# Summing weight blocks inside the transfer: accumulating loads in place of VectorE adds in a seven-product feed-forward

## The chip, the cores and the metric

The kernel runs on one core of one Trainium2 chip. The metric is the device time of one execution in microseconds (us). The granted clock of TensorE is given as a share of its full speed of 2.4 GHz.

## The reference

Two decoder layers over 256 tokens of width 2048, all in float32. Layer 0 has differential attention, layer 1 multi-head latent attention; each is followed by a dense SwiGLU feed-forward with 5632 hidden columns. Only the second product of the feed-forward matters for the change:

```
def _swiglu(h, w_in, w_out):
    g, u = jnp.split(h @ w_in, [FFN_HIDDEN], axis=-1)
    return (jax.nn.silu(g) * u) @ w_out

for i in range(DEPTH):
    ...
    y = _swiglu(_rmsnorm(x, g[2]), ffn_w_in[i], ffn_w_out[i])
    x = x + _rmsnorm(y, g[3])
```

## The kernel before

Each float32 product is made of three matmuls over a high and a low part (`mm3`, lines 94 to 100): high x high, high x low, low x high. A weight piece of 128 x 2048 float32 (1 MB) is loaded by SyncE and split in two halves by `split_weight` (lines 81 to 92): for each half ScalarE casts the high part (`whi`, line 103) and VectorE subtracts it to get the low part (`wlo`, line 104). The pools of `whi` and of `wlo` hold six halves each, so three pieces can be split or in use at one time; the pool of loaded pieces `w` holds two, that of raw output-weight blocks `wr` three.

In a feed-forward (`ffn`, from line 461) the hidden columns come in 11 blocks of 512. `block_in` projects one block: eight pieces of `win`, 24 matmuls each, and after each of them it yields. Blocks 0 to 9 form five pairs. For a pair and two groups of 512 output columns, `unit` (from line 555) computes a 2 x 2 product of blocks (two token tiles by two hidden blocks, times two hidden blocks by two column groups) with seven block products in place of eight. The sums on the side of the hidden values are the operands A11, S1, S2, S4, S3, A12 and A22; the sums on the side of the weights are made in the tiles t1 and t3:

```
t1 = W[b1,n1]                       product 1 (A11)
t1 += W[b1,n2]                      product 2 (S1)
t1 += W[b2,n2]                      product 3 (S2)
W[b2,n2] itself                     product 4 (S4)
t3 = W[b1,n2] + W[b2,n2]            product 5 (S3)
W[b2,n1] itself                     product 6 (A12)
t1 += W[b2,n1]                      product 7 (A22)
```

Each product is 12 matmuls of 512 columns. The raw blocks t1, t3, b22 and b21 are loaded by SyncE (`raw`, line 561). One step of a unit runs at each yield of `block_in`, so one projection piece and one product alternate on TensorE. There are two units to a pair and five pairs to a layer, 20 units in the kernel; the last unit of each layer runs when no block is left to project, among the products of the single eleventh block (lines 652 to 675).

The order of instructions on each engine is made by the planner when the kernel is built, from the order of the program and its own estimate of durations; on the chip each engine then takes its instructions in that order and waits where data or a buffer is missing. GpSimd does only the small steps of the norms (`rsqrt_mean`, lines 119 to 125) once its tables are made.

Of the kernel before, what the change touches and what calls it, by code (L numbers as in the profile page):

```python
# [14 lines left out]
ALU = mybir.AluOpType  # L15
# [24 lines left out]
def trunk_kernel(ctx: ExitStack, tc: tile.TileContext, a: dict):  # L40
    nc = tc.nc
# [39 lines left out]
    def split_weight(w, shape, parts=1):  # L81
        both = []
        half = shape[0] // 2
        for h in range(2):
            hi = whi.tile([P, half] + shape[1:], F32R, tag="whi", name="whi")
            lo = wlo.tile([P, half] + shape[1:], F32R, tag="wlo", name="wlo")
            n = half // parts
            for i in range(parts):
                c = slice(i * n, (i + 1) * n)
                split_to(hi[:, c], lo[:, c], w[:, h * half + i * n : h * half + (i + 1) * n])  # L90
            both += [(hi[:, i], lo[:, i]) for i in range(half)]
        return both
# [368 lines left out]
    def ffn(i, rstd, second_tokens, first_tokens, aside=None):  # L461
        win, wout = a[f"win{i}"], a[f"wout{i}"]
# [87 lines left out]
        def product(ps, lhs, rhs, more=False):  # L550

            for k in range(4):
                mm3(ps, (lhs[0][:, k], lhs[1][:, k]), rhs[k], not more and k == 0, k == 3, more)

        def unit(pair, X, cgs, first):

            (b1, b2), (n1, n2) = pair, cgs

            def raw(blk, cg):
                w = wr.tile([P, 4, CW], F32, tag="r", name="wr")  # L560
                nc.sync.dma_start(w, wout[blk, cg])
                return w

            def split(w):
                return split_weight(w, [4, CW])

            def add(into, w):
                nc.vector.tensor_tensor(into, into, w, op=ALU.add)  # L568

            def sums():  # L570
                return wp.tile([P, CW], F32, tag="wp", name="wp")

            def ys(t, cg):
                return y[:, t, cg * CW : (cg + 1) * CW]

            def gather(t, cg, ps, sign, fresh=False):
                if fresh:
                    nc.scalar.mul(ys(t, cg), ps, sign)
                else:
                    op = ALU.add if sign > 0 else ALU.subtract  # L580
                    nc.vector.tensor_tensor(ys(t, cg), ys(t, cg), ps, op=op)  # L581

            t1 = raw(b1, n1)
            pa = sums()
            product(pa, X["A11"], split(t1))
            gather(0, n1, pa, 1.0, first)
            yield
            t3 = raw(b1, n2)
            add(t1, t3)
            pc = sums()  # L590
            product(pc, X["S1"], split(t1))
            gather(1, n2, pc, -1.0, first)
            yield
            b22 = raw(b2, n2)
            add(t1, b22)
            product(pa, X["S2"], split(t1), more=True)
            gather(0, n2, pa, -1.0, first)
            yield
            product(pc, X["S4"], split(b22), more=True)
            gather(0, n2, pc, -1.0)  # L600
            yield
            add(t3, b22)
            product(pa, X["S3"], split(t3), more=True)
            gather(1, n2, pa, -1.0)
            yield
            b21 = raw(b2, n1)
            pc = sums()
            product(pc, X["A12"], split(b21))
            gather(0, n1, pc, 1.0)
            yield  # L610
            add(t1, b21)
            product(pa, X["A22"], split(t1), more=True)
            gather(1, n1, pa, 1.0, first)
            yield
# [17 lines left out]
        for blk in range(NBLK):  # L632
            if blk == NBLK - 1:
                A, hidden = single_operands()
            elif blk % 2 == 0:
                X, hidden, second = pair_operands()
            else:
                hidden = second
            for _ in block_in(blk, hidden):
                next(steps, None)  # L640
            drain(steps)
            if blk == 2 and aside is not None:
                aside()
            if blk % 2 == 1:
                waiting = (PAIRS[blk // 2], X, blk == 1)
                steps = unit(waiting[0], waiting[1], (0, 1), waiting[2])
            elif waiting is not None:
                steps = unit(waiting[0], waiting[1], (2, 3), waiting[2])
# [355 lines left out]
```

## Time and profile before

| | |
|---|---|
| median of three runs | 2126.69 us (2126.25 to 2127.41) |
| the profiled execution: its own time | 2126.84 us |
| its span, first to last instruction | 2125.1 us |
| TensorE busy | 2077.7 us (98%) |
| VectorE busy | 1584.2 us (75%) |
| ScalarE busy | 1123.2 us (53%) |
| GpSimd busy | 45.5 us (2%) |
| moved by DMA | 394.97 MB, mean 186 GB/s |

Busy time is the time in which an engine executes something; a share of the whole span hides that stages have different limits. In the chain of work that ended last, TensorE holds 92% of the span, VectorE 5% and DMA 2%.

### The profile page before, as it was taken

To read this page: it belongs to the slowest core of one execution; us is meant where nothing else is said; L and a number is where in the kernel's file an instruction comes from. 1 tells how busy PE (TensorE), PEld (TensorE's weight loads), DVE (VectorE), ACT (ScalarE), POOL (GpSimd) and SP (SyncE) were. 2 spreads that over 40 slices of the span, in tenths; PEclk is the share of its full clock that TensorE was granted. 3 is DMA by queue.
4 is the path that set the end of the run, shared out by engine and by line. 5 is a ranking of instruction groups with operands and counts; after the bars stand their busy time and mean duration, and the time that the engine had idled before them with its cause. 6 is when DMAs were issued, how large, how long until landed. Compare 5 with 4: busy or idle time off the path is not lost.

```text
span 2125.1 us, 26154 instructions
## 1 busy us (share of the span) xinstructions
PE 2077.7 (98%) x10348; PEld 1770.9 (83%) x10348; DVE 1584.2 (75%) x1757; ACT 1123.2 (53%) x1439; POOL 45.5 (2%) x83
## 2 busy tenths in 40 slices
PE   8999999999999999999998999999999999999997
PEld 7999998788888888888877898878888888888875
DVE  6655555657878888887887786475888878888887
ACT  6444444455555555555555654454555555555554
POOL 0000000000000000000001100000000000000000
PEclk9999999999999999999999999999999999999998
DMA  7555456454556555566534533645455556555552
GB/s 248 179 174 175 162 179 229 167 198 144 213 201 224 189 181 198 188 220 223 182 114 151 198 138 135 237 162 194 179 174 190 207 208 219 195 177 196 189 202 94
DMA packets 59452, 394.97 MB, mean 186 GB/s; under 512 B 7105, under 2 KB 7361, under 8 KB 13633
## 3 DMA queue, kind: packets, MB, share of 16 engines
q1 hardware_dynamic: 59328, 393.30, 53.0%
q8 instruction: 81, 1.33, 0.3%
q14 instruction: 43, 0.34, 0.0%
HBM read 391.17 MB, written 2.10 MB: 185 GB/s over the span
## 4 chain that ended last, share of the span: by engine, by line
PE 92%; DVE 5%; DMA 2%; issue 1%; ACT 1%; POOL 0%; SPq 0%; DVEq 0%; POOLq 0%; ACTq 0%
PE ps L98 24%; PE ps L100 24%; PE ps L99 24%; PE wp L99 5%; PE wp L100 5%; PE wp L98 5%; DVE wlo L104 2%; PE pt L494 1%; DVE x L262 1%; PE pt L110 1%; PE ps_s L863 0%; PE ps_s L389 0%; PE ps_s L864 0%; PE po L428 0%; ACT whi L103 0%
## 5 line engine op out<-in xcount | busy, mean ns | idle before, releaser
L104 DVE TENSOR_TENSOR wlo<-w,whi 128x1024 fp32r<-128x1024 f32 (+3 forms) x582 | 697.7, 1205 | 300.5 <-ACT whi L103 282.3
L103 ACT CAST whi<-w 128x1024 fp32r<-128x1024 f32 (+3 forms) x582 | 600.5, 1039 | 509.7 <-PE ps L100 246.6
L98 PE MATMUL ps<-whi,xTh 128*128 128x512 f32 (+2 forms) x1632 | 631.8, 390 | 1.3 <-ACT xTh L103 1.3
L99 PE MATMUL ps<-wlo,xTh 128*128 128x512 f32 (+2 forms) x1632 | 631.9, 387 | 0.0
L100 PE MATMUL ps<-whi,xTl 128*128 128x512 f32 (+2 forms) x1632 | 631.8, 387 | 0.0
L103 ACT CAST whi<-wr 128x1024 fp32r<-128x1024 f32 x280 | 293.2, 1051 | 302.0 <-PE ps L100 268.3
L104 DVE TENSOR_TENSOR wlo<-wr,whi 128x1024 fp32r<-128x1024 f32 x280 | 340.1, 1223 | 124.0 <-ACT whi L103 112.2
L98 PEld LDWEIGHTS ps<-whi,xTh 128*128 128x128 f32 x1632 | 308.3, 189 | 61.9 <-ACT xTh L103 2.4
L100 PEld LDWEIGHTS ps<-whi,xTl 128*128 128x128 f32 x1632 | 307.9, 189 | 60.4 <-DVE xTl L104 0.2
L99 PEld LDWEIGHTS ps<-wlo,xTh 128*128 128x128 f32 x1632 | 308.3, 189 | 59.9 <-DVE wlo L104 0.4
L568 DVE TENSOR_TENSOR wr<-wr 128x2048 f32<-128x2048 f32 x80 | 182.8, 2285 | 23.5 <-DMA wr<-in_wout 23.3
L98 PE MATMUL ps<-xTh,whi 128*128 128x256 f32 x512 | 146.8, 287 | 1.6 <-ACT whi L103 1.6
L100 PE MATMUL ps<-xTh,wlo 128*128 128x256 f32 x512 | 144.8, 283 | 0.8 <-DVE wlo L104 0.8
L99 PE MATMUL ps<-xTl,whi 128*128 128x256 f32 x512 | 144.8, 283 | 0.0
L98 PEld LDWEIGHTS ps<-xTh,whi 128*128 128x128 f32 x512 | 98.2, 192 | 2.2 <-ACT whi L103 2.0
L98 PE MATMUL ps<-whi,oTh 128*128 128x512 f32 x256 | 100.0, 393 | 0.0
L100 PE MATMUL ps<-whi,oTl 128*128 128x512 f32 x256 | 99.2, 390 | 0.0
L99 PE MATMUL ps<-wlo,oTh 128*128 128x512 f32 x256 | 99.2, 390 | 0.0
L100 PEld LDWEIGHTS ps<-xTh,wlo 128*128 128x128 f32 x512 | 98.1, 192 | 1.1 <-DVE wlo L104 1.0
L99 PEld LDWEIGHTS ps<-xTl,whi 128*128 128x128 f32 x512 | 98.2, 192 | 0.2
L581 DVE TENSOR_TENSOR y<-y,wp 128x512 f32<-128x512 f32 x124 | 84.4, 681 | 3.7 <-PE wp L100 3.7
L98 PE MATMUL wp<-whi,S_S 128*128 128x512 f32 x160 | 63.7, 398 | 5.7 <-ACT whi L103 5.7
(210 smaller groups left out, 2358.2 us busy)
## 6 DMA issues: line engine op xcount, KB each, us to landing
w<-in_win SPq DMA_DIRECT2D x176, 1024.0 KB, 4.9
wr<-in_wout SPq DMA_DIRECT2D x80, 1024.0 KB, 4.9
w<-in_wqk SPq DMA_DIRECT2D x32, 1024.0 KB, 4.9
w<-in_wo SPq DMA_DIRECT2D x32, 1024.0 KB, 4.9
w<-in_wv SPq DMA_DIRECT2D x15, 1024.0 KB, 4.9
w<-in_wout SPq DMA_DIRECT2D x8, 1024.0 KB, 5.1
w<-in_wdown SPq DMA_DIRECT2D x8, 724.0 KB, 4.3
g<-in_norm_gains SPq DMA_DIRECT2D x16, 256.0 KB, 3.6
```

The costliest lines, as they stand in the source:

```text
L98: nc.tensor.matmul(out, lh, rh, start=first, stop=False, skip_group_check=more)
L99: nc.tensor.matmul(out, lh, rl, start=False, stop=False, skip_group_check=more)
L100: nc.tensor.matmul(out, ll, rh, start=False, stop=last, skip_group_check=more)
L103: nc.scalar.copy(hi, src)
L104: nc.vector.tensor_tensor(lo, src, hi.bitcast(F32), op=ALU.subtract)
L110: nc.tensor.transpose(pt[:, j * P : (j + 1) * P], src[:, j * P : (j + 1) * P], ident)
L262: nc.vector.scalar_tensor_tensor(xs, y[:, t, cg * CW : (cg + 1) * CW], ry, xs, op0=ALU.mult, op1=ALU.add)
L494: nc.tensor.transpose(pt[:, j * P : (j + 1) * P], hs[t][:, j * P : (j + 1) * P], ident)
L568: nc.vector.tensor_tensor(into, into, w, op=ALU.add)
L581: nc.vector.tensor_tensor(ys(t, cg), ys(t, cg), ps, op=op)
```

## The change

The helper `add` in `unit` no longer adds one loaded tile into another on VectorE. It issues a transfer from GpSimd's queue that reads the block from memory and adds it to what the destination tile holds. The tiles that are also used by themselves (t1, t3, b22, b21) are still loaded as before, so the four blocks that enter a sum are read from memory once more for each sum.

```diff
-            def add(into, w):
-                nc.vector.tensor_tensor(into, into, w, op=ALU.add)
+            def add(into, blk, cg):
+
+                nc.gpsimd.dma_start(into, wout[blk, cg], accum_op=ALU.add)
...
             t3 = raw(b1, n2)
-            add(t1, t3)
+            add(t1, b1, n2)
...
             b22 = raw(b2, n2)
-            add(t1, b22)
+            add(t1, b2, n2)
...
-            add(t3, b22)
+            add(t3, b2, n2)
             product(pa, X["S3"], split(t3), more=True)
...
-            add(t1, b21)
+            add(t1, b2, n1)
             product(pa, X["A22"], split(t1), more=True)
```

## Rows read from the trace of the kernel before

**Rows 1.** The core's span and its mean granted clock.
```profile
core 0: 2125.1 us, clock 0.990
```
**Rows 2.** Busy time by stretch: a whole unit, and both layers' ends.
```profile
core 0: us, PE busy (x) PEld busy (x) DVE busy (x) ACT busy (x) POOL busy (x), PEclk, DMA share, GB/s
...
812.00:875.00 63.00, 63.00 (x283) 52.27 (x283) 51.78 (x46) 34.42 (x37) 0.00 (x0) 1.00 0.57 198
...
1062.00:1092.00 30.00, 26.40 (x107) 21.25 (x106) 26.15 (x25) 13.67 (x15) 0.00 (x0) 0.89 0.37 134
...
2052.00:2082.00 30.00, 26.40 (x114) 21.39 (x113) 26.59 (x24) 13.68 (x15) 0.00 (x0) 0.94 0.38 133
```
**Rows 3.** What TensorE waited for, 1060 to 1125: total, times, longest.
```profile
PE wp L98 <- ACT whi L103: 2.8, 1, 2.8
PE wp L99 <- DVE wlo L104: 0.8, 1, 0.8
```
**Rows 4.** The group of the adds on the page.
```profile
L568 DVE TENSOR_TENSOR wr<-wr 128x2048 f32<-128x2048 f32 x80 | 182.8, 2285 | 23.5 <-DMA wr<-in_wout 23.3
```
**Rows 5.** DMA from 812 to 875: queue, and issues with us to landing.
```profile
q1 hardware_dynamic: 1709, 12.43, 56.6%
...
w<-in_win SPq DMA_DIRECT2D x8, 1024.0 KB, 4.8
wr<-in_wout SPq DMA_DIRECT2D x4, 1024.0 KB, 4.8
```
**Rows 6.** Landing times of all 80 raw blocks (line 561).
```profile
DMA to landing us min/median/max: 4.7/4.9/11.8
```
**Rows 7.** Durations of GpSimd's small norm step, ns min/median/max.
```profile
L122 POOL TENSOR_SCALAR ms<-so x20: 190/274/3277, 89.2 to 1190.9; 128x1 f32<-128x1 f32 x20
```
**Rows 8.** VectorE in order of time, products 1 and 2 of a unit.
```profile
816.66 1.22 DVE L104 TENSOR_TENSOR wlo<-wr,whi 128x1024 fp32r<-128x1024 f32 x1
...
818.58 2.28 DVE L568 TENSOR_TENSOR wr<-wr 128x2048 f32<-128x2048 f32 x1
...
825.91 2.53 DVE L104 TENSOR_TENSOR wlo<-wr,whi 128x1024 fp32r<-128x1024 f32 x2
...
829.71 2.29 DVE L568 TENSOR_TENSOR wr<-wr 128x2048 f32<-128x2048 f32 x1
```
**Rows 9.** ScalarE: the first casts of products 2 and 3.
```profile
824.76 1.05 ACT L103 CAST whi<-wr 128x1024 fp32r<-128x1024 f32 x1 [3.07 <-PE ps L100]
...
833.82 1.05 ACT L103 CAST whi<-wr 128x1024 fp32r<-128x1024 f32 x1 [0.61 <-PE ps L100]
```
**Rows 10.** TensorE: the first matmuls of products 2 and 3.
```profile
834.93 0.39 PE L98 MATMUL wp<-whi,S_S 128*128 128x512 f32 x1
...
843.09 0.39 PE L98 MATMUL wp<-whi,S_S 128*128 128x512 f32 x1
```
**Rows 11.** VectorE at the end of the first layer.
```profile
1066.04 2.59 DVE L104 TENSOR_TENSOR wlo<-wr,whi 128x1024 fp32r<-128x1024 f32 x2 [2.48 <-ACT whi L103]
1068.66 2.29 DVE L568 TENSOR_TENSOR wr<-wr 128x2048 f32<-128x2048 f32 x1
...
1074.33 2.35 DVE L104 TENSOR_TENSOR wlo<-wr,whi 128x1024 fp32r<-128x1024 f32 x2
...
1080.13 2.28 DVE L568 TENSOR_TENSOR wr<-wr 128x2048 f32<-128x2048 f32 x1
```
**Rows 12.** TensorE there: products 2 and 3 of the last unit.
```profile
1076.99 0.39 PE L98 MATMUL wp<-whi,S_S 128*128 128x512 f32 x1
...
1083.60 0.50 PE L98 MATMUL wp<-whi,S_S 128*128 128x512 f32 x1 [2.84 <-ACT whi L103]
1084.86 0.79 PE L99 MATMUL wp<-wlo,S_S 128*128 128x512 f32 x1 [0.76 <-DVE wlo L104]
```
**Rows 13.** The chain that ended last, 1079 to 1092: start, us, piece.
```profile
1086.50 0.43 PE wp L99
...
1091.32 0.23 PE wp L99
```

## The prediction

> **What bounds the kernel now.** I read the cores first: one core, span 2125.1 us, granted clock 0.99 [rows 1], which is the upper level, 2.4 GHz, nearly throughout. Then the table by stretches. In a stretch of the first feed-forward layer that holds one whole seven-product unit, TensorE is busy 63.00 of 63 us at clock 1.00, VectorE 51.78, ScalarE 34.42, and the 16 DMA engines 0.57 of the time; of the stretches with units only those at the ends of the two layers leave TensorE short, 26.40 of 30 us each, at clock 0.89 and 0.94 [rows 2]. The reader is to see that VectorE's load is no bound in the middle of a layer: there is no time there that a lighter VectorE could give back. The waits of TensorE say what the ends cost: 2.8 us for a cast and 0.8 us for a subtraction in each [rows 3]. That and a stretch of matmuls at the lower clock level are all that this change can win.
>
> **What it removes.** 80 VectorE adds of 2.285 us, 182.8 us of VectorE [rows 4]; four in each of 20 units (5 pairs x 2 units x 2 layers). Of these units 18 run between the projection pieces of a block, and 2 (the last of each layer) run bare at a layer's end. In the middle the 9.1 us of adds per unit hide behind a TensorE that never waits, so removing them is worth 0 there; were VectorE the bound, it would be worth up to those 9.1 us a unit.
>
> **What it adds.** 80 transfers of 1 MB into a tile that already holds data, issued by GpSimd: 83.9 MB on top of 395 MB. One unit's stretch now carries 12 loads (8 and 4 of 1 MB) in 56.6% of 63 us [rows 5], so one load holds the 16 engines for 0.566 x 63 / 12 = 3.0 us, and lands 4.8 us after issue, 1.8 us of which is fixed. The trace has no accumulating transfer. Bounds of its latency L, from the last read of the tile to the sum being there: below, the fastest plain landing, 4.7 us, if the second operand costs nothing and GpSimd starts as fast as SyncE; above, the slowest plain landing, 11.8 us [rows 6], with a second operand (3.0) and GpSimd's slowest small instruction as its start (3.3, median 0.27) [rows 7]: 18.1 us. I take: fixed 1.8, engine time 6.0 (the old content of the tile has to be fetched as well as the block, so twice 3.0), 3.4 for other loads that get in meanwhile (0.566 of 6.0), and 1.0 for GpSimd's start: L = 12.2 us. I take twice, not once, because two operands of 1 MB must pass; nothing in the rows argues for more.
>
> In the Trainium skill, *Collectives: The Full Stack*, section "The bandwidth ceiling: the fold count and why AG ≠ RS ≠ AR", a reduction done by the DMA engines runs at half the rate of a copy since it reads two sources, and the addition itself costs nothing. No row here shows that; by it the 6.0 stands, by the plain row's 3.0 alone L would be 7.5 and the middle would cost nothing. *DMA: Bandwidth & Descriptors*, section "Measured (HBM→SBUF, 128 partitions, SWDGE, issued from GpSimd)", gives 6.15 us of engine span for 1 MB issued from GpSimd, descriptor writing not counted, against this trace's 4.8 from SyncE to landing. With that in place of 4.8, L would be 13.5 us and the end some 2279 us, as an estimate from that page, inside the forecast's own range below.
>
> **What waits for it.** The tile t1 holds the first, second, third and seventh weights in turn, so the second and third sums form a chain: subtraction of product 1's split ends, sum, split, sum, split. In the stretch above, product 1's split ends at 816.66 + 1.22 = 817.9, the adds run at 818.58 and 829.71, and the split between them subtracts from 825.91 to 828.44 [rows 8]. The casts of products 2 and 3 start at 824.76 and 833.82 [rows 9]; their first matmuls at 834.93 and 843.09 [rows 10], one step of 8.16 us apart. From a cast's start to the end of the first half's subtraction is 2.4 us (824.76 to 827.2), to the end of the second half's 3.7 (to 828.44). So there is cover: the splits run ahead of TensorE by most of a step. With sums that land L after the last read, product 3 can start on time if 817.9 + L + 3.7 + L + 2.4 is no later than 843.3 (its second matmul is the first to need a subtracted half), so if 2L is at most 19.3, L at most 9.65 us. Product 2 alone would bear L = 14.8. The last add on t1, product 7's, has four more steps and stays hidden; so does the one into t3, which no earlier product reads.
>
> At L = 12.2 each unit comes 2 x 12.2 - 19.3 = 5.1 us late at product 3; 18 units: 92 us. What queues behind the late cast on ScalarE is the next projection piece's cast, which is later by as much and has the same cover, so I add nothing for it; without that cover each such piece would be a second wait. Behind the waiting transfers on GpSimd's queue stands nothing in the middle (GpSimd is idle there); at the ends the norm's small steps come after the last sum. SyncE's loads keep their order; a load delayed by sharing costs nothing while it lands ahead of its cast.
>
> **The ends.** Here the products follow one another with no projection between, and the DMA engines are nearly idle (0.37 and 0.38 of the stretch [rows 2]), so L is 1.8 + 6.0 + 1.0 = 8.8. Before, product 1's subtraction ends at 1068.6, the first add follows at once, the split's at 1076.7, and the second add, queued behind other VectorE work, ends at 1082.4 [rows 11]. Product 2 starts at 1076.99; product 3 is late, 1083.60, with another 0.76 us lost behind it [rows 12]. After: first sum at 1077.4, product 2 at about 1079.8, its split done 1081.1, second sum 1089.9, product 3 at 1092.3, 8.7 us later. Product 4 and the single block's product can fill some of that if the planner puts them ahead; and VectorE is lighter by three adds. TensorE's matmuls after the wait came 0.43 us apart, the lower level of 1.2 GHz, until 1091, then 0.23, at 2.4 GHz [rows 13]; a longer wait makes that no better. I count +5 us an end, +10 in all (bounds 0 and +12 each).
>
> **Sum.** 92 + 10 = +102 us on the profiled execution's 2126.84 us (span 2125.1 and 1.7 around it, 0.15 above the runs' median): 2229 us.
>
> **The rivals.**
> *The DMA engines become the bound.* A unit's loads hold them for 12 x 3.0 + 4 x 6.0 = 60 of 62.6 us already. If one sum holds them for more than 6.7 us, they cannot keep up whatever the order. At 9.0: L = 1.8 + 9.0 + 5.1 + 1.0 = 16.9, 14.5 us a unit, 261 us and 15 at the ends: 2403 us. For it: 0.57 before; against it: nothing shows an addition to cost more than its two operands.
> *The sums stay hidden.* L at most 9.65: the middle is free, and the ends cost 0 to 10 us: 2127 to 2137 us, within 0.2% at L below about 6. For it: the fastest landing is 4.7 and the engines have gaps; against it: a second operand and a second issuer, both above nothing.
> *Faster.* One mechanism: at the ends VectorE is freed of three adds, the late second add (5.7 us after its tile was free) turns into a sum that arrives sooner, and the 3.6 us of waits with some 3 us lost at the lower level go, twice: -13 us, 2114 us. It decides where two sums take less than the 2.3 + 5.7 = 8.0 us of the two adds with their queueing, so L under 4.0, below the fastest plain landing; only a better order of TensorE's work at the ends helps it beyond that.
> *The change does not do what it says:* excluded, since the adds can only leave VectorE.
>
> **How the numbers follow.** Forecast (late by some us in each unit) 0.60; DMA engines the bound 0.20; hidden within 0.2% 0.12; faster 0.08. So faster 0.08, same 0.12, slower 0.80; 0.2%, 4 us, is about what a measurement of this kernel tells from no change. The likeliest case's own range runs from L = 10 (0.7 x 18 + 10) to L = 15 (10.7 x 18 + 14): 2150 to 2333. Each us of L is worth 36 us, so the whole range is wide: from the hidden case, 2124, to the upper bound of L, 18.1 (16.9 x 18 + 20 = 324), 2450; it leaves out the faster case but for its edge, and the worst of the second, together under 0.2.
>
> **What would show it.** VectorE's line of adds gone, its busy time near 1401 us; a second DMA queue with 84 MB; a landing time near 12 us for the accumulating transfers; a cast of t1's tile waiting for that queue in nearly every unit, twice, and TensorE waiting at product 3, some 5 us, in the middle of the layers, where it never waited; DMA share near 0.9 there. Wrong it would be through L: under 9.65 the middle shows no wait at all, above 15 every unit waits more than 10 us. It would also be wrong if the planner orders TensorE's products so that others fill the wait.

## The result and the profile after

The changed kernel takes 2155.25 us (median of 4, 2154.14 to 2158.2) against 2126.48 us for the kernel before: 1.0137 times, with an interval of 1.0119 to 1.0154, or 28.8 us slower. The forecast was 102 us slower. The profiled execution took 2155.12 us, its span 2153.3 us.

Queues, the casts' and the sums' groups, and the issues, on the page after:
```profile
q1 hardware_dynamic: 59328, 393.30, 49.0%
q0 software_dynamic: 11520, 83.89, 20.7%
...
L103 ACT CAST whi<-wr 128x1024 fp32r<-128x1024 f32 x280 | 287.0, 1049 | 385.4 <-DMA wr<-in_wout 220.6
...
L569 POOL DMA_DIRECT2D wr<-in_wout x80 | 68.9, 861 | 1442.1 <-DVE wlo L104 1095.7
...
wr<-in_wout SPq DMA_DIRECT2D x80, 1024.0 KB, 8.0
wr<-in_wout POOLq DMA_DIRECT2D x80, 1024.0 KB, 9.2
```
A second queue carries 83.89 MB. Its packets took 20.7% of 16 engines' span, so one sum holds the 16 engines for 0.207 x 2153.3 / 80 = 5.57 us. A sum lands 9.2 us after its issue (7.8 at the least, 13.5 at the most), and ScalarE's casts stand 220.6 us before it. The plain loads suffer too: a raw block lands after 8.0 us, not 4.9 [rows 6]. VectorE's busy time fell from 1584.2 to 1405.8 us.

The stretches, columns as in [rows 2]: a whole unit, the first layer's end, most of that layer's middle, and the time behind its end, the last once more for the kernel before:
```profile
812.00:875.00 63.00, 63.00 (x283) 52.24 (x283) 42.63 (x42) 33.33 (x37) 3.44 (x4) 1.00 0.85 263
1062.00:1092.00 30.00, 22.42 (x95) 17.75 (x93) 14.12 (x16) 8.31 (x10) 2.58 (x3) 0.91 0.77 187
...
500.00:1060.00 560.00, 558.99 (x2498) 462.23 (x2497) 383.25 (x386) 303.52 (x330) 29.95 (x35) 1.00 0.85 261
...
1092.00:1122.00 30.00, 25.05 (x90) 19.46 (x91) 21.76 (x23) 15.49 (x19) 0.86 (x1) 0.80 0.45 132
```
```profile
1092.00:1122.00 30.00, 29.99 (x133) 24.51 (x132) 25.37 (x28) 15.48 (x22) 0.00 (x0) 1.00 0.36 122
```
The unit's stretch has lost 9.15 us of VectorE and gained 0.28 of DMA share, and TensorE is busy throughout as before. In 560 us of the layer's middle it misses 1.0 us, where it missed none before. At the layer's end it misses 7.6 us of 30, where it missed 3.6 before, and behind that the granted clock is 0.80 in place of 1.00.

What TensorE waited for from 1060 to 1125, the stretch of [rows 3]:
```profile
PE wp L98 <- ACT whi L103: 10.2, 2, 7.0
PE ps L98 <- ACT whi L103: 1.8, 1, 1.8
PE wp L99 <- DVE wlo L104: 0.5, 1, 0.5
```
So the waits there grew from 3.6 to 12.5 us. Four points in time split the whole loss:

| start of | before, us | after, us | later by |
|---|---|---|---|
| product 1 of the first layer's last unit | 1074.27 | 1075.91 | 1.6 |
| the second layer's first projection | 1134.74 | 1146.79 | 12.1 |
| product 1 of the second layer's last unit | 2063.67 | 2078.25 | 14.6 |
| the span's end | 2125.1 | 2153.3 | 28.2 |

The 18 middle units (with the attention between) cost 1.6 + 2.5 = 4.1 us; the two ends, 10.5 and 13.6, cost 24.1. The forecast had it the other way round: 92 and 10. Part of the ends' 24.1 us is no wait. Before, TensorE was busy for 49.01 us from product 1 of the first layer's last unit to the second layer's projection, and for 44.17 us from product 1 of the second layer's last unit to the end; now it is 52.48 and 48.90 us for the same matmuls (in these stretches the granted clock is 0.89 and 0.89 before, 0.84 and 0.83 after). That is 3.5 and 4.7 us of slower matmuls; the other 16 us are waits. The second end, before and after:
```profile
2063.67:2125.10 61.43, 44.17 (x189) 35.43 (x187) 49.27 (x59) 23.94 (x36) 1.84 (x4) 0.89 0.26 90
```
```profile
2078.25:2153.30 75.05, 48.90 (x189) 38.62 (x187) 44.90 (x56) 26.19 (x38) 3.56 (x6) 0.83 0.40 111
```

**A middle unit, link by link.** A link is the time from the end of one split of t1 to the cast that begins the next; in it lie the issue of the sum and its landing. VectorE's last pieces of product 1's and product 2's splits, GpSimd's issues, ScalarE's casts, TensorE's first matmuls of products 2 and 3 (start, duration, engine, line; idle time and its releaser in brackets):
```profile
880.14 1.22 DVE L104 TENSOR_TENSOR wlo<-wr,whi 128x1024 fp32r<-128x1024 f32 x1
...
893.36 1.22 DVE L104 TENSOR_TENSOR wlo<-wr,whi 128x1024 fp32r<-128x1024 f32 x1
```
```profile
881.76 0.86 POOL L569 DMA_DIRECT2D wr<-in_wout  x1 [11.46 <-DVE wlo L104]
894.98 0.86 POOL L569 DMA_DIRECT2D wr<-in_wout  x1 [12.36 <-DVE wlo L104]
```
```profile
890.53 2.00 ACT L103 CAST whi<-wr 128x1024 fp32r<-128x1024 f32 x2 [5.37 <-DMA wr<-in_wout]
...
903.06 2.00 ACT L103 CAST whi<-wr 128x1024 fp32r<-128x1024 f32 x2 [6.06 <-DMA wr<-in_wout]
```
```profile
898.41 0.39 PE L98 MATMUL wp<-whi,S_S 128*128 128x512 f32 x1
...
906.57 0.39 PE L98 MATMUL wp<-whi,S_S 128*128 128x512 f32 x1
```
The reader is to see both casts released by the sum's landing, and both matmuls without a bracket: the casts wait, TensorE doesn't. Product 1's split ends at 881.36, so the first link is 890.53 - 881.36 = 9.2 us; product 2's split ends at 894.58, so the second is 8.5. Together 17.7 us, under the 19.3 that the cover bears, with 1.6 to spare. This unit is one of the easier ones: counted to the landing of each sum, the two links come to 18.6 us in the median of the 18 middle units, from 16.3 to 19.3, so L is 9.1 us on average and the whole middle runs just inside its cover. The first link is mostly the longer (median 9.6 us, the second 8.5). Product 3's first matmul at 906.57 is still one step of 8.16 us behind product 2's at 898.41.

**The first layer's end, link by link.** The same four engines:
```profile
1067.67 2.59 DVE L104 TENSOR_TENSOR wlo<-wr,whi 128x1024 fp32r<-128x1024 f32 x2 [2.47 <-ACT whi L103]
...
1082.03 2.36 DVE L104 TENSOR_TENSOR wlo<-wr,whi 128x1024 fp32r<-128x1024 f32 x2 [5.09 <-ACT whi L103]
```
```profile
1062.12 0.85 POOL L569 DMA_DIRECT2D wr<-in_wout  x1 [25.10 <-DVE wlo L104]
1070.66 0.88 POOL L569 DMA_DIRECT2D wr<-in_wout  x1 [7.69 <-DVE wlo L104]
1084.80 0.85 POOL L569 DMA_DIRECT2D wr<-in_wout  x1 [13.25 <-DVE wlo L104]
```
```profile
1080.95 1.99 ACT L103 CAST whi<-wr 128x1024 fp32r<-128x1024 f32 x2 [11.37 <-DMA wr<-in_wout]
...
1093.56 2.94 ACT L103 CAST whi<-wr 128x1024 fp32r<-128x1024 f32 x3 [8.24 <-DMA wr<-in_wout]
```
```profile
1082.05 0.51 PE L98 MATMUL wp<-whi,S_S 128*128 128x512 f32 x1 [3.26 <-ACT whi L103]
...
1094.66 0.79 PE L98 MATMUL wp<-whi,S_S 128*128 128x512 f32 x1 [6.97 <-ACT whi L103]
1095.92 0.79 PE L99 MATMUL wp<-wlo,S_S 128*128 128x512 f32 x1 [0.47 <-DVE wlo L104]
```
From split to cast it takes 1080.95 - 1070.26 = 10.7 us and 1093.56 - 1084.39 = 9.2 us, and no cover stands over them: TensorE waits 3.26 and 6.97 us for the two casts. With the 1.6 us by which the unit began later taken off, product 2 starts at 1080.4 and product 3 at 1093.1; the forecast for them was 1079.8 and 1092.3.

The first GpSimd issue shown, at 1062.12, is the sum into t3, which no product waits for yet. It lands 12.9 us later, at 1075.1, so it is still under way for 4.4 us when product 2's sum follows at 1070.66 on the same queue and lands after 10.2 us. In the ends-only kernel below, where t3's sum had landed 0.9 us before product 2's was issued, product 2's landed after 8.4 us.

### The profile page after: what moved, and what is told of

It reads as the page before. It is cut to its first block, busy times and chain, and to the rows that moved or that the text cites. A ratio compares the mean times of both kernels' runs of the same rounds, so it can differ in the third digit from the quotient of the medians.

```text
span 2153.3 us, 26376 instructions
## 1 busy us (share of the span) xinstructions
PE 2088.1 (97%) x10348; PEld 1774.3 (82%) x10348; DVE 1405.8 (65%) x1677; ACT 1106.6 (51%) x1439; POOL 112.6 (5%) x163
## 3 DMA queue, kind: packets, MB, share of 16 engines
q0 software_dynamic: 11520, 83.89, 20.7%
## 4 chain that ended last, share of the span: by engine, by line
PE 85%; DMA 7%; DVE 5%; ACT 2%; issue 1%; POOL 0%; SPq 0%; DVEq 0%; POOLq 0%; ACTq 0%
PE ps L99 22%; PE ps L98 22%; PE ps L100 22%; DMA wr<-in_wout 6%; PE wp L100 5%; PE wp L98 5%; PE wp L99 5%; DVE wlo L104 3%; ACT whi L103 1%; PE pt L110 1%; PE pt L494 1%; DVE x L262 1%; PE ps_s L864 0%; PE ps_s L389 0%; PE ps_s L865 0%
## 5 line engine op out<-in xcount | busy, mean ns | idle before, releaser
L103 ACT CAST whi<-w 128x1024 fp32r<-128x1024 f32 (+3 forms) x582 | 594.5, 1037 | 502.9 <-PE ps L100 208.3
L103 ACT CAST whi<-wr 128x1024 fp32r<-128x1024 f32 x280 | 287.0, 1049 | 385.4 <-DMA wr<-in_wout 220.6
L569 POOL DMA_DIRECT2D wr<-in_wout x80 | 68.9, 861 | 1442.1 <-DVE wlo L104 1095.7
```

The lines of the kernel that those rows point to most:

```text
L103: nc.scalar.copy(hi, src)
L569: nc.gpsimd.dma_start(into, wout[blk, cg], accum_op=ALU.add)
```

## The experiments

Two theories. In the expectations A is the chain: two sums in a row stand between the splits of t1, a unit loses 2L - 19.3 us at product 3 where that is positive, and the ends lose nearly all that their chain is late by. B is the rival of the run at hand, in several of them that the load of 83.9 MB more on the DMA engines sets the time, whatever the order. All edits are in `add`, which is called here with the other tile and the product's number as well; LAST stands for the last unit of a layer. Each time is a median, compared with the kernel before on the same chip (2126.4 to 2126.6 us).

**The middle alone and the ends alone.**
```diff
+                if not LAST:                   # e1; e5: if LAST
                     nc.gpsimd.dma_start(into, wout[blk, cg], accum_op=ALU.add)
+                else:
+                    nc.vector.tensor_tensor(into, into, w, op=ALU.add)
```


> Accumulating transfers in the 18 units that run between projections; VectorE adds, as before, in the last unit of each layer. Theory A (the loss sits at the ends: by the start times of the last units and of what follows them, the middle cost 1.6 + 2.8 us and the ends 10.4 + 13.6): some 2131 us, 4 to 5 us above the kernel before, and the ends' product 3 late by 2.8 us as before the change. Theory B (84 MB more on the shared DMA engines slow the whole feed-forward, and the ends only show it last): 2140 us or more.

> The reverse of the first experiment: accumulating transfers only in the last unit of each layer, VectorE adds in the other 18. Theory A (the ends carry the loss): 28.8 - 7.7 = 21 us above the kernel before, 2147 us, with product 3 waiting some 7 us at each end. Theory B (the ends only show a backlog that the traffic of the middle built up): under 10 us above it.

Measured: the middle alone 2134.18 us, 1.0035 (1.0023 to 1.0048), +7.7; the ends alone 2144.45 us, 1.0089 (1.0075 to 1.0103), +18.0. The two add up to 25.7 of the 28.8. So 72 transfers in the middle cost 0.4 us a unit, and the 8 transfers at the ends 9 us an end. TensorE's waits in the ends-only kernel, 1060 to 1125:
```profile
PE wp L98 <- ACT whi L103: 9.8, 2, 8.4
PE ps L98 <- ACT whi L103: 1.4, 1, 1.4
PE wp L99 <- DVE wlo L104: 0.5, 1, 0.5
```
They come to 11.7 us, near the 12.5 of the full change, with the longer one at product 3; the middle's traffic isn't needed for them. What the full change adds at the ends is slower matmuls. In the ends-only kernel TensorE is busy for 49.62 and 45.95 us in the two stretches from the last unit's product 1 on, 0.6 and 1.8 us more than before, against 3.5 and 4.7 in the full change: 5.8 us, about the difference between the ends' 24.1 us there and 18.0 here. There product 2, too, waits 3.26 us (at 1082.05), and its matmuls behind that come 0.40 us apart on average (1083.31 to 1087.29); here it waits 1.42 us, and they come 0.24 us apart (1079.64 to 1082.04).

In the middle-only kernel the waits that exist are like this one, in a unit whose first link took 705.28 - 693.28 = 12.0 us from issue to cast:
```profile
718.61 0.51 PE L98 MATMUL wp<-whi,S_S 128*128 128x512 f32 x1 [0.36 <-ACT whi L103]
719.87 0.51 PE L99 MATMUL wp<-wlo,S_S 128*128 128x512 f32 x1 [0.76 <-DVE wlo L104]
```
Product 3 is the place that the rule names. Of the 18 units, three have two links of more than 20 us together, counted to the landings (20.5, 20.5 and 21.0), and just these three wait at product 3 for 0.7 us or more (0.75, 0.76 and 1.1). TensorE's gaps in its two middle stretches (500 to 1060 and 1500 to 2066) add up to 1.6 + 2.9 = 4.5 of the 7.7 us; the other 3 us were not placed.

**What the addition costs and what GpSimd's queue costs.** The same transfers, plain, so that the sums are left out:
```diff
-                nc.gpsimd.dma_start(into, wout[blk, cg], accum_op=ALU.add)
+                nc.gpsimd.dma_start(into, wout[blk, cg])
```


> The four transfers of each unit are issued by GpSimd to the same tiles at the same places, but overwrite instead of adding, so the sums are left out. It measures what the addition costs inside the transfer. If the second operand costs engine time (theory A: 5.6 us for an accumulating, 2.8 us for a plain MB): landing 6 to 6.5 us instead of 9.2, the new queue's share 10% instead of 21%, ends 5 us shorter each, 2140 us. If the issuer is what costs (theory B): landing 8 to 9 us, time as changed, 2155 us.

Measured: 2127.95 us, 1.0008 (0.9998 to 1.0017). Queues and issues on its page:
```profile
q1 hardware_dynamic: 59328, 393.30, 52.5%
q0 software_dynamic: 11520, 83.89, 11.2%
...
wr<-in_wout SPq DMA_DIRECT2D x80, 1024.0 KB, 5.0
wr<-in_wout POOLq DMA_DIRECT2D x80, 1024.0 KB, 5.2
```
The bytes read from memory, the waits and the chain are those of the change, and no cost shows; the 2140 expected was too much. One transfer holds the engines for 0.112 x 2125.9 / 80 = 2.98 us and lands after 5.2 us. So the addition, and not the traffic or the issuer, makes the difference: it adds 4.0 us to the landing and makes the engine time 5.57 / 2.98 = 1.87 times as long. GpSimd as issuer costs 0.3 us beside SyncE's 4.9 [rows 6].

**A longer chain in the middle.** The middle-only kernel, with a second transfer behind each chained sum, of 64 columns (e4) or whole (e12), so that these columns are added twice:
```diff
                 nc.gpsimd.dma_start(into, wout[blk, cg], accum_op=ALU.add)
+                if product in (2, 3):          # e12: whole tiles
+                    nc.gpsimd.dma_start(into[:, 0, 0:64], wout[blk, cg][:, 0, 0:64], accum_op=ALU.add)
```


> As the first of this set (middle units only), but behind each of the two chained sums a second accumulating transfer of 64 columns into the same tile, waiting for the first, so 64 columns are added twice. It lengthens L by a small transfer's issue and landing, some 2.7 us, with next to no traffic. By the prediction's rule (product 3 is late by 2L - 19.3; the trace now shows 2L = 17.7) 2L becomes some 23: 3.7 us late in each of 18 units, 67 us above the first of this set, 2198 us (2160 to 2230). Rival (the planner's order or ScalarE's queue hides any such wait): no more than 10 us above it.

> As the fourth experiment, with a whole second accumulating transfer (the block is added twice) behind each of the two chained sums of the 18 middle units. 2L becomes some 35.5 us. By the prediction's rule alone product 3 is 16.2 us late in each unit: 292 us above the first experiment, 2426 us. With the cost that the fourth experiment showed beside the wait (matmuls at the lower clock level after it, some 3 us a unit): 345 us, 2480 us. If the DMA engines become the bound instead (12 x 2.8 + 6 x 5.6 = 67 of 63 us): no more than 100 us, 2234 us.

Measured: 2271.6 us, 1.0679 (1.0664 to 1.0693), 137 us over the middle-only kernel; and 2467.37 us, 1.1603 (1.1588 to 1.1619), 333 us over it. The stretch 500 to 1060 of e4 and then of e12 (columns as in [rows 2]):
```profile
500.00:1060.00 560.00, 518.52 (x2209) 422.06 (x2208) 339.72 (x338) 270.13 (x292) 40.12 (x47) 0.95 0.77 232
```
```profile
500.00:1060.00 560.00, 460.68 (x1903) 370.22 (x1902) 294.61 (x293) 233.03 (x254) 35.23 (x41) 0.90 0.79 223
```
A small transfer lands in 2.5 us (2.3 at the least), and the 36 of them move 1.2 MB in all, yet TensorE, which missed 1.6 us there, misses 41.5. The DMA share went down, from 0.84 in the middle-only kernel to 0.77 and 0.79. Load can't do this; a longer chain does. That refutes the rival of the DMA engines as the bound, for which e12 was at most 2234 us. (Its condition was not met either: a sum holds the engines for 5.57 us, not for more than 6.7.)

The rule alone gave about half of e4's loss, with 2L put at 23 us. Measured from the splits' ends to the landings 2L is 24.7 us on average (23.6 to 26.9), for which the rule gives 5.4 us a unit; the waits measured around product 3 are 4.8 (3.8 to 6.9). So the rule prices the wait fairly. What it leaves out is seen behind a wait, TensorE's matmuls and then the chain that ended last (start, us, piece) of e4:
```profile
887.69 0.80 PE L98 MATMUL wp<-whi,S_S 128*128 128x512 f32 x1 [4.46 <-ACT whi L103]
888.95 0.80 PE L99 MATMUL wp<-wlo,S_S 128*128 128x512 f32 x1 [0.46 <-DVE wlo L104]
```
```profile
891.45 0.43 PE wp L98
...
894.01 0.43 PE wp L99
...
894.70 0.23 PE ps L99
```
After a wait of 4.46 us the matmuls come 0.43 us apart, the level of 1.2 GHz, for some 5.5 us, and then 0.23 again, the level of 2.4 GHz: about 13 matmuls by 0.2 us, 2.6 us that are no wait. Per unit e4's 137 / 18 = 7.6 us are 4.6 of waits (80.8 + 12.1 us in e4 less 6.0 + 4.0 in e1, over 18) and 3.0 without, near that. For e12 the rule gave 292 us, and with this cost 345; 333 were measured.

**Only the sums that nobody waits for.** Products 2 and 3 get VectorE's add back; products 5 and 7 keep the transfer, in all units (e2) or in the last ones alone (e9):
```diff
+                if product in (5, 7):          # e9: and LAST
                     nc.gpsimd.dma_start(into, wout[blk, cg], accum_op=ALU.add)
+                else:
+                    nc.vector.tensor_tensor(into, into, w, op=ALU.add)
```


> In every unit, only the sums of products 5 and 7 come by accumulating transfer; those of products 2 and 3, the chain, are VectorE adds. Theory A (a sum hurts only where a split waits for it at once): no loss, 2120 to 2127 us, and at each end the second add is no longer queued behind the add into t3, so product 3 is up to 2.3 us earlier there. Theory B (traffic): half of the extra transfers, half of the loss, some 2140 us.

> Accumulating transfers only for products 5 and 7 of the last unit of each layer (4 in all); everything else is VectorE adds as before the change. If the 3.5 us that the second experiment won lie at the ends, where VectorE is short: 2122 to 2124 us. If they lie in the 18 units of the middle: 2126 us.

Measured: 2122.89 us, 0.9985 (0.9976 to 0.9994), and 2122.64 us, 0.9983 (0.9974 to 0.9992). Both beat the kernel before by some 3.7 us, four transfers as much as 40. So the gain lies at the ends, and a VectorE that is lighter in the middle is worth nothing. VectorE's second add, and TensorE's waits from 1060 to 1125, in e2:
```profile
1074.65 2.28 DVE L571 TENSOR_TENSOR wr<-wr 128x2048 f32<-128x2048 f32 x1
```
```profile
PE ps L98 <- ACT whi L103: 2.0, 1, 2.0
PE wp L99 <- DVE wlo L104: 1.3, 2, 0.8
```
The second add, queued until 1080.13 before [rows 11], runs at 1074.65, and the wait of 2.8 us for product 3's cast [rows 3] is gone. A wait of 2.0 us comes up at a projection's matmul.

**Halves.** Each sum as two transfers of half a block, as each split already goes by halves:
```diff
+                for h in range(2):
+                    c = slice(h * 2, h * 2 + 2)
+                    nc.gpsimd.dma_start(into[:, c], wout[blk, cg][:, c], accum_op=ALU.add)
```


> The changed kernel with each sum made by two accumulating transfers of half a block, so that a half can be summed while the other is still split. A half holds the engines 2.8 us, so the first cast can start some 6.5 us after the read of its half (1.8 fixed, 2.8, and 1.5 to 2 of sharing) instead of 9.2. By theory A (only the latency of the chain costs) the two links shorten by some 3 us each: the middle's 7.7 us go, the ends lose 10 us each less 4 to 6: 2135 us (2128 to 2142). If the traffic and its packets cost (theory B): no better than the changed kernel, 2155 us.

Measured: 2131.34 us, 1.0023 (1.0014 to 1.0032), 24 us faster than the change.
```profile
q0 software_dynamic: 23040, 83.90, 22.5%
...
wr<-in_wout POOLq DMA_DIRECT2D x160, 512.0 KB, 6.5
```
The bytes are the same and the engine time is no less (0.225 x 2129.6 / 80 = 6.0 us a sum). What is shorter is the chain: a half lands in 6.5 us, where a whole block took 9.2. TensorE has no wait at all from 500 to 1060, and at the first layer's end 2.5, 2.3 and 1.5 us. The chain sets the time, not the load.

**Another order at the ends.** Product 4 ahead of product 3 in the last unit, and the single block's first piece with it; with the full change (e6), with e2's sums (e8), and with VectorE's adds throughout (e10):
```diff
             add(t1, b2, n2, b22, 3)
-            product(pa, X["S2"], split(t1), more=True)
...
             product(pc, X["S4"], split(b22), more=True)
             gather(0, n2, pc, -1.0)
             yield
+            product(pa, X["S2"], split(t1), more=True)
...
+        next(steps)
```


> The changed kernel with another order in the last unit of each layer: products 1, 2, 4, then the single block's first piece, then 3, 5, 6, 7. The sum is the same; 8.2 us of TensorE's work stand between products 2 and 3. The prediction counted on the planner for part of this. If the ends are lost to a wait that nothing fills (theory A): product 3's wait of 7 us goes, and with it some of the lower clock, 7 to 9 us an end: 2140 us. If the ends are lost to what comes after product 3 as well, the buffers and loads that follow it (theory B): under 5 us an end, 2147 us or more.

> Accumulating transfers only for products 5 and 7 (as in the second experiment, 2122.9 us) together with the new order in the last units. The wait at product 3 there is 0.3 us at most already, so the order can only help what follows; 2118 to 2123 us if the add into t1 has been the late one, 2125 us if moving product 4 ahead makes the block b22 late.

> The kernel before with the new order in the last units (1, 2, 4, the single block's first piece, 3, 5, 6, 7) and no accumulating transfer. If the eighth experiment's further 2.1 us come from the order alone: 2124 us; if the order is of use only with a lighter VectorE: 2126 us.

Measured: 2146.53 us, 1.0102 (1.0088 to 1.0115); 2120.75 us, 0.9973 (0.9963 to 0.9983); 2124.76 us, 0.9992 (0.9983 to 1.0001). In e6 the planner put product 3's first matmul ahead of product 4's all the same:
```profile
1099.30 0.80 PE L98 MATMUL wp<-whi,S_S 128*128 128x512 f32 x1 [7.22 <-ACT whi L103]
...
1099.89 0.63 PE L98 MATMUL wp<-whi,S 128*128 128x512 f32 x1
```
So the wait of 7.22 us was not filled, and how much of it product 4 could fill stays open. Where the 8.7 us that e6 gains over the change come from stays open too: the profiled execution took 2152.34 us, and the other three 2145.4 to 2146.9. With e2's sums the order gives about 2 us more, and 1.7 by itself; neither is clear of its interval. e8 is the fastest version here, 5.6 us under the kernel before.

**VectorE's chained adds in halves,** on top of e2:
```diff
+                for h in range(2):
+                    c = slice(h * 2, h * 2 + 2)
+                    nc.vector.tensor_tensor(into[:, c], into[:, c], w[:, c], op=ALU.add)
```


> As the second experiment (products 5 and 7 by transfer), but the VectorE adds of products 2 and 3 are made in two halves, so that the first half can be cast one half add (1.15 us) earlier. Theory A (at the ends the chain through t1 counts): 2 x 1.15 us at each of two ends, 2118 to 2121 us. If VectorE's sum of work counts there: 2123 us or a little more, since each half pays its own start.

Measured: 2122.33 us, 0.9979 (0.9971 to 0.9988): no gain over e2 that can be told from none. Halving a link of 2.3 us does not do what halving one of 9.2 us did.

## Why the prediction was right in direction and wrong in place and size

The direction was right by the smaller of its two terms: the ends, put at 10 us, cost 18 to 24, and the middle, put at 92, cost 4 to 8. The case it called hidden was right about the middle and too low at the ends.

1. *The middle gives nothing back to a lighter VectorE.* Right: TensorE is full before and after, and e9 equals e2.
2. *The engine time of a sum is that of two operands, 6.0 us.* Nearly right: 5.57. The Trainium skill, *Collectives: The Full Stack*, section "The bandwidth ceiling: the fold count and why AG ≠ RS ≠ AR", says that a reduction by the DMA engines runs at half the rate of a copy, and the trace agrees with 1.87 times the plain transfer's 2.98.
3. *L = 12.2 us in the middle.* **This is the step that failed.** The mis-sized term is that of the other loads. The fixed part and the engine time were fair: 1.8 + 5.57 + 0.3 for GpSimd makes 7.7 from issue to landing, and the fastest sum landed after 7.8. From the last read to the issue another 0.4 us pass (881.36 to 881.76), so GpSimd's start, taken as 1.0, is 0.7, and 8.1 us are accounted for. The chained sums of the middle took 9.1 on average: the other loads were given 3.4 us and took some 1.0. I had let every load that is due meanwhile in ahead of the sum; the loads came late as well (raw blocks after 8.0 us, not 4.9), which costs nothing while they land ahead of their casts. L of 9.1 lies just under the threshold of 9.65, so 92 us became 4 to 8. The forecast named this point and gave "hidden" a chance of 0.12, too low for a threshold inside the bounds of L.
4. *The rule, 2L - 19.3 at product 3.* Its place and its threshold were right: waits at product 3, none at 17.7 us, small ones above 20 us in e1, 4.8 us a unit at 24.7 us in e4. Its price was short: a wait of some us is followed by matmuls at 1.2 GHz that cost nearly 3 us more.
5. *The ends: product 3 8.7 us late, but only 5 counted.* The lateness was near (9.5 measured), with some luck: the links took 10.7 and 9.2 us in place of 8.8 each, but product 3's first matmul came 1.1 us behind its cast, where the forecast had reckoned 2.4. The discount was wrong, and is the second step that failed: nothing filled the wait, since the planner kept its order (product 4 and the single block's product still come behind product 3), and the lower clock, put at nothing, came on top with 8.2 us. Uncut, 2 x 8.7 = 17.4 us stands beside e5's 18.0. The DMA engines are as free of other loads there as was said: from 1060 to 1092 the plain loads' queue has 28.1% of their time, where it had 35.3% before. The rise to 0.77 is the sums' own queue with 49.4%, and what was left out is that t3's sum runs beside product 2's.
6. *The sum,* +102: with L below the threshold, and the ends uncut, the same working gives +17 us, against +28.8; the slower matmuls at the ends (8.2 us) and the middle (4.1 us) make up about the rest.
7. *The rivals.* DMA engines the bound: refuted by e12 and by the 5.57 us of a sum. Faster by a freed VectorE at the ends: not for this change, where the chain is longer than the adds it replaces; but its mechanism is real and shows in e2, once the chained sums are left alone. The Trainium skill's 6.15 us for 1 MB issued from GpSimd (*DMA: Bandwidth & Descriptors*, section "Measured (HBM→SBUF, 128 partitions, SWDGE, issued from GpSimd)") was not borne out: 5.2 us from issue to landing in e3, 2.98 of it engine time.

## What to carry to other kernels

Ask of each operation that is moved to a transfer whether the next step waits for it: a transfer trades an engine's 2.3 us for some 9 us of latency, which is free for the sums that have steps to spare and dear for two in a row that nothing covers, and halving the transfer shortens the chain where the bytes stay the same. Where a cost is a threshold (late only above 2L = 19.3), a bound that straddles it makes two forecasts and not one: give both a real chance. Do not discount a wait because other work could fill it; look whether the order of that work is fixed.

## What the runs showed of the hardware

- A 1 MB transfer that adds into its destination holds the 16 DMA engines for 5.57 us and lands in 9.2 us (7.8 at best); the plain one from the same queue takes 2.98 and 5.2 us. Two halves of it land in 6.5 us each.
- GpSimd's instruction for such a transfer took 861 ns, that of the plain one 535 ns (e3).
- An addition of 64 columns alone lands after 2.5 us (2.3 to 4.1), in e4.
- A wait of 4.5 us in a stretch of dense matmuls was followed by 5.5 us at half the clock (e4, 887.69). At the two ends of the changed kernel the same matmuls kept TensorE busy 3.5 and 4.7 us longer than before.
